# Sixteen experts taken in groups of four in the down product, and the 48 dense chunks of a second stream tied to places among their loads

## The chip, the cores and the metric

One core of a Trainium2 chip. The metric is the device time of one execution in microseconds, the median of several runs. TensorE, VectorE (DVE), ScalarE (ACT), GpSimd (POOL) and the sync engine (SP) each have a queue of their own and work through it in order; sixteen DMA engines carry what SP, POOL and ACT issue.

## The reference, cut to what matters

Two networks one behind the other over 256 tokens of width 1024, all in 32-bit floats. The first has one block: a linear-attention mixer, then a mixture of 16 experts. Each expert picks its own 32 tokens:

```python
gate, idx = lax.top_k(jnp.swapaxes(aff, 1, 2), cap)              # 16 experts, 32 tokens each
xe = h[bidx, idx]
a = jnp.einsum('becd,edf->becf', xe, w_gate)                     # 1024 -> 1408
u = jnp.einsum('becd,edf->becf', xe, w_up)
ye = jnp.einsum('becf,efd->becd', jax.nn.silu(a) * u, w_down) * gate[..., None]
return jnp.zeros_like(h).at[bidx, idx].add(ye)
```

The second network has two layers of four mixers and an MLP (1024 to 4096 and back), on the tokens and on a context of 256 positions of its own. The context's stream does not depend on the first network: its whole first layer, and keys and values of its second, can be computed at any time before the tokens reach the layer that reads them.

## The kernel before, in words

An expert's weights come in loads of 704 KB (128 partitions of 1408 numbers, `load_raw`, L271): eight for gate, eight for up, eight for down. SP issues all 384 in program order into a ring of six buffers (`ringp`); the first 16 go into buffers of their own ahead of the experts (`load_ahead`, L801). SP's order is the program's; the order on every other engine is made by a planner, which walks through the program with a modelled timeline and puts on each engine what is ready there, earlier lines first.

`up_and_gate` (L1045) multiplies an expert's 32 gathered tokens with a load in four products of 352 columns, each of which runs as two instructions, so a load is eight instructions of L1057. The four products go to four strips of 32 columns of the array. Then `sgm` (tanh on ACT, two operations on DVE) and a transpose on DVE give the hidden values `ht` (L1087 to L1091).

The down product (L1095 to L1106) takes eight rounds `c`, one for each 128 output columns. A round is one load: eleven products of 128 columns, 22 instructions of L1101, spread over the four strips and accumulated to four partial sums. ACT evacuates them (`ye`), a product with `ga` (L1105, two instructions) adds the four partial sums, weighs them and scatters the 32 tokens to their 256 places, and DVE adds the result to `xT` (L1106). `ga` is made for each expert: POOL copies the expert's 32 columns of `oa` four times (L1080), TensorE transposes (L1082), ACT evacuates. In the last expert each round also feeds the sums of squares for the next norm (L1110 to L1113).

The context's stream (`ZF`, L1499) stands behind the experts in the program: `layer(ZF, 0, ...)`, then `k_chunk` and `v_chunk` for the second layer (L1501 to L1507). It has 48 calls of `dense` (L287): 10 in the mixers, 4 in their output product, 16 and 16 in the MLP, 2 for the last keys and values. A call has 48 products of 256 columns (L305). Its weights come in two halves of 512 KB, issued on POOL's queue into three buffers (`fr`); ACT splits off the high part (`hi`, L265), DVE or, in the mixers and for keys and values, POOL the low part (`lo`, L267), into three pairs of buffers (`hlp`). As the planner's order goes by what is ready, the context's products come in wherever the experts' products wait, from the first expert on. Its mixers hold long chains on DVE and ACT: 62 taps of a convolution (L1303), softmax, norms.

After the experts the tokens go through the two layers of the second network (`ZC`); these read the context's keys and values.

Of the kernel before, what the change touches and what calls it, by code (L numbers as in the profile page):

```python
# [10 lines left out]
FT = mybir.dt.float32  # L11
# [7 lines left out]
T = 256  # L19
# [84 lines left out]
def layout(inp):  # L104
# [78 lines left out]
    dn = f("w_exp_down")[0].reshape(NE, 128, 11, 8, 128).transpose(0, 3, 1, 2, 4)  # L183
    a["wd"] = np.ascontiguousarray(dn).reshape(NE, 8, 128, RW)
# [20 lines left out]
def build(tc, I, out, dbg=None, upto=99):  # L205
# [35 lines left out]

    def advance(n):

        for _ in itertools.islice(fills[0], n):
            pass
# [41 lines left out]
    def dense(ps, parts, H, act_stationary=False, order=(0, 1), fill=0, late=False, n=0):  # L287

        hh, hl_ = H
        for rnd in ((0, 1), (2,)) if late else ((0, 1, 2),):
            for half in order:
                whi, wlo = parts[half]
                pairs = ((whi, hh), (wlo, hh), (whi, hl_)) if late else ((whi, hh), (whi, hl_), (wlo, hh))
                for k in range(4):
                    kk = half * 4 + k
                    for b in range(2):
                        s = slice(b * 128, (b + 1) * 128)
                        for w, h in (pairs[i] for i in rnd):  # L300
                            if act_stationary:
                                l, r = h[:, kk, s], w[:, k, :]
                            else:
                                l, r = w[:, k, s], h[:, kk, :]
                            PE.matmul(ps[:, b, :], l, r, start=(n == 0), stop=(n == 47), skip_group_check=True)  # L305
                            n += 1
                    if fill and k % 2:
                        advance(fill)

# [735 lines left out]
    def up_and_gate(e):  # L1045
# [5 lines left out]
        for w, ps in ((I["wg"], pg), (I["wu"], pu)):  # L1051
            for k in range(KD):
                if e == 0 and ps is pg and k < KD - 1:
                    gather(k + 1)
                raw = ahead.pop(0) if ahead else load_raw(ZA, w[e, k], RW)
                for j in range(4):
                    PE.matmul(ps[32 * j:32 * j + 32, :], xe[:, k, e * 32:(e + 1) * 32],  # L1057
                              raw[:, j * 352:(j + 1) * 352], start=(k == 0), stop=(k == KD - 1))
# [15 lines left out]
    for e in range(NE):  # L1074
        pg, pu = pgpu if e == 0 else up_and_gate(e)

        pga = pdn.tile([128, 512], FT, name="pga", tag="dn")
        o4 = tb.tile([128, 2, 128], FT, name="o4", tag="o4")
        for a in range(2):
            G.tensor_copy(o4[:, a, :].rearrange("p (j s) -> p j s", j=4),  # L1080
                          oa[:, a, None, e * 32:(e + 1) * 32].to_broadcast([128, 4, 32]))
            PE.transpose(pga[:, a * 128:(a + 1) * 128], o4[:, a, :], ident)  # L1082
        ga = tb.tile([128, T], FT, name="ga", tag="ga")
        evac(ga, pga[:, :T])
# [5 lines left out]
        ht = tb.tile([128, 11, 32], FT, name="ht", tag="ht")  # L1090
        V.transpose(ht, sgm.rearrange("p (q i) -> p i q", i=11))  # L1091
        if e == NE - 1:
            sums = pgu.tile([128, 352], FT, name="sums", tag="pg")

        for c in range(8):  # L1095
            pd = pdn.tile([128, 512], FT, name="pd", tag="dn")
            py, po = pd[:, 0:128], pd[:, 256:512]
            raw = load_raw(ZA, I["wd"][e, c], RW)
            for i in range(11):
                j = i % 4  # L1100
                PE.matmul(py[32 * j:32 * j + 32, :], ht[:, i, :], raw[:, i * 128:(i + 1) * 128], start=(i < 4),  # L1101
                          stop=(i >= 7))
# [4 lines left out]
            if e == NE - 1:  # L1107
# [375 lines left out]
    def layer(Z, l, mod, m, x, norm1=norm):  # L1483
# [16 lines left out]
                x=c2T, np=3, ahead=0, lo=G, fill=0, sc=fms, sct="ms")  # L1500
    ZF.dma.dma_start(c2T.rearrange("p k t -> p (k t)"), I["c2T"])  # L1501
# [5 lines left out]
    v_chunk(ZF, 1, H, vc[1])  # L1507
    phF.close()
# [67 lines left out]
```

## Time and profile before

| | us |
|---|---|
| median of 3 runs | 1938.36 |
| lowest, highest | 1932.96, 1942.03 |
| the profiled execution | 1939.22 |
| its span, first to last instruction | 1937.3 |
| TensorE busy | 1735.1 (90%) |
| DVE busy | 1020.8 (53%) |
| ACT busy | 652.1 (34%) |
| POOL busy | 432.1 (22%) |

Bytes moved: 529.36 MB, on average 273 GB/s. The granted clock of TensorE over the span is 0.919 of full speed. Busy time is a union of overlapping instructions; a busy TensorE is not TensorE at its peak. In a table of stretches, (x...) is the number of instructions, PEld is the loading of stationary operands, "DMA share" the mean busy share of the 16 DMA engines (it can read slightly over 1).

### The profile page before, as it was taken

The numbers are of one execution on the slowest core, as the hardware profiler recorded it, in microseconds if no ns is written. First come the engines' busy times: TensorE is split into PE (matmuls) and PEld (weight loads), VectorE is DVE, ScalarE is ACT, GpSimd is POOL, SyncE is SP. The second block draws the span as 40 slices with busy tenths as digits, with TensorE's granted clock in tenths as the row PEclk, the third lists the DMA queues.
The fourth block names the chain that finished last, engine by engine and source line by source line (L and its number), as shares of the span: only waits on it lengthen the run. The fifth ranks groups of instructions, "written<-read, shape, count | busy, mean of one in ns | idle before, by whom it ended". The sixth has DMA issues, their size and how long they took to land. (4 is left out here: it accounts for less than half of the span.)

```text
span 1937.3 us, 37898 instructions
## 1 busy us (share of the span) xinstructions
PE 1735.1 (90%) x15947; PEld 1353.1 (70%) x15947; DVE 1020.8 (53%) x1892; ACT 652.1 (34%) x1095; POOL 432.1 (22%) x408
## 2 busy tenths in 40 slices
PE   5998998879989999998878777889899999989998
PEld 3776876456667776776533322677899897789997
DVE  5666564556445343434311111538688884867664
ACT  3432332313323222223200000235454343545443
POOL 2334131464321011101200000254411125540000
PEclk8999998889999999999967676789999999999999
DMA  9667887788799999999899999742368863335651
GB/s 356 222 220 241 321 295 258 287 322 286 260 349 344 375 374 360 363 356 367 326 414 414 414 407 413 275 146 89 109 219 319 297 213 96 112 109 163 186 185 66
DMA packets 124232, 529.36 MB, mean 273 GB/s; under 512 B 13917, under 2 KB 14173, under 8 KB 123550
## 3 DMA queue, kind: packets, MB, share of 16 engines
q1 hardware_dynamic: 91086, 405.56, 56.8%
q0 software_dynamic: 32544, 119.16, 17.9%
q8 instruction: 125, 2.05, 0.4%
q10 hardware_dynamic: 432, 2.23, 0.3%
q14 instruction: 45, 0.37, 0.0%
HBM read 525.84 MB, written 1.05 MB: 272 GB/s over the span
## 5 line engine op out<-in xcount | busy, mean ns | idle before, releaser
L265 ACT ACTIVATE hi<-raw 128x1024 fp32r<-128x1024 f32 x316 | 329.4, 1054 | 317.7 <-PE oproj L305 109.8
L267 POOL TENSOR_TENSOR lo<-raw,hi 128x1024 fp32r<-128x1024 f32 x94 | 239.6, 2558 | 471.0 <-ACT hi L265 406.2
L267 DVE TENSOR_TENSOR lo<-raw,hi 128x1024 fp32r<-128x1024 f32 x222 | 273.1, 1243 | 106.4 <-ACT hi L265 104.5
L305 PE MATMUL oproj<-hidh,hi 128*128 128x256 f32 x768 | 218.8, 285 | 8.5 <-ACT hi L265 5.7
L305 PE MATMUL oproj<-hidh,lo 128*128 128x256 f32 x768 | 219.3, 286 | 7.2 <-DVE lo L267 7.2
L305 PE MATMUL oproj<-hidl,hi 128*128 128x256 f32 x768 | 217.8, 284 | 0.0
L305 PE MATMUL pw<-hh,hi 128*128 128x256 f32 x704 | 202.2, 290 | 8.4 <-ACT hi L265 3.1
L305 PE MATMUL pw<-hh,lo 128*128 128x256 f32 x704 | 201.5, 290 | 6.0 <-DVE lo L267 6.0
L305 PE MATMUL pw<-hlo,hi 128*128 128x256 f32 x704 | 194.5, 287 | 1.6 <-DVE hlo L360 1.6
L305 PEld LDWEIGHTS oproj<-hidh,hi 128*128 128x128 f32 x768 | 146.4, 191 | 18.3 <-ACT hi L265 9.8
L305 PEld LDWEIGHTS oproj<-hidh,lo 128*128 128x128 f32 x768 | 146.0, 190 | 14.7 <-DVE lo L267 9.5
L305 PEld LDWEIGHTS oproj<-hidl,hi 128*128 128x128 f32 x768 | 145.8, 190 | 6.9 <-issue 6.9
L1057 PE MATMUL pu<-raw,xe 128*32 128x352 f32 x1024 | 131.7, 599 | 21.1 <-DMA raw<-in_wu_dram 21.1
L1106 DVE SCALAR_TENSOR_TENSOR xT<-pd,mod,xT 128x256 f32<-128x256 f32 x128 | 61.3, 483 | 166.6 <-PE pd L1105 165.9
L305 PEld LDWEIGHTS pw<-hh,hi 128*128 128x128 f32 x704 | 136.3, 194 | 17.4 <-ACT hi L265 5.4
L305 PEld LDWEIGHTS pw<-hh,lo 128*128 128x128 f32 x704 | 136.1, 194 | 12.6 <-DVE lo L267 8.0
L1057 PE MATMUL pg<-raw,xe 128*32 128x352 f32 x1024 | 116.4, 524 | 25.6 <-DMA raw<-in_wg_dram 25.4
L305 PEld LDWEIGHTS pw<-hlo,hi 128*128 128x128 f32 x704 | 132.3, 193 | 9.7 <-issue 7.7
L1101 PE MATMUL pd<-raw,ht 128*32 128x128 f32 x2816 | 115.6, 293 | 20.4 <-DVE ht L1091 10.6
L609 ACT ACTIVATE ye<-pd 128x128 f32<-128x128 f32 x128 | 35.2, 276 | 285.0 <-PE pd L1101 284.7
L1101 PEld LDWEIGHTS pd<-raw,ht 128*32 128x32 f32 x2816 | 88.1, 116 | 53.4 <-issue 28.2
L479 DVE CUSTOM_DVE_ANT_0 raw<-raw,adarow,par 128x1024 f32<-128x1024 f32 x64 | 84.0, 1313 | 59.8 <-DMA raw<-in_ada0x_dram 40.0
(460 smaller groups left out, 3572.8 us busy)
## 6 DMA issues: line engine op xcount, KB each, us to landing
raw<-in_wg_dram SPq DMA_DIRECT2D x128, 704.0 KB, 7.4
raw<-in_wu_dram SPq DMA_DIRECT2D x128, 704.0 KB, 8.4
raw<-in_wd_dram SPq DMA_DIRECT2D x128, 704.0 KB, 7.9
raw<-in_w_dram SPq DMA_DIRECT2D x128, 512.0 KB, 3.9
raw<-in_wi_dram SPq DMA_DIRECT2D x68, 512.0 KB, 5.4
raw<-in_ada_dram POOLq DMA_DIRECT2D x64, 512.0 KB, 4.9
raw<-in_w_dram POOLq DMA_DIRECT2D x64, 512.0 KB, 7.3
raw<-in_ada0x_dram POOLq DMA_DIRECT2D x32, 512.0 KB, 4.9
```

Of the source, the lines that this page charges most:

```text
L265: A.activation(hi, src, AF.Copy, scale=scale)
L267: (eng or V).tensor_sub(lo, src, hi.bitcast(FT))
L305: PE.matmul(ps[:, b, :], l, r, start=(n == 0), stop=(n == 47), skip_group_check=True)
L479: V.tensor_tensor_reduce(raw, raw, row, 1.0, bias[:, 16 + n:17 + n], OP.mult, OP.add, accum_out=mod[:, 0, 16 + n:17 + n])
L609: A.activation(dst, ps, AF.Copy, scale=scale)
L1057: PE.matmul(ps[32 * j:32 * j + 32, :], xe[:, k, e * 32:(e + 1) * 32], raw[:, j * 352:(j + 1) * 352], start=(k == 0), stop=(k == KD - 1))
L1101: PE.matmul(py[32 * j:32 * j + 32, :], ht[:, i, :], raw[:, i * 128:(i + 1) * 128], start=(i < 4), stop=(i >= 7))
L1106: V.scalar_tensor_tensor(xT[:, c, :], po, m0[:, 0, 40 + c:41 + c], xT[:, c, :], op0=OP.mult, op1=OP.add)
```

## The change

The down weights are laid out anew on the host, so that a load holds 11 of the 44 blocks of 128x128 that four experts have for one round. The experts are taken in groups of four: gate and up of all four with their hidden values, then eight rounds of four loads. In a round the four experts' products go to the four strips, 44 in all, so the evacuated tile holds 4 x 32 tokens, and one product with `ga` scatters them. `ga` is now the plain transpose of 128 columns of `oa`; the copies on POOL are gone. `ht` has eight buffers instead of two.

The last TensorE instruction of each of the 384 loads is kept in `steps`. From these 48 are chosen, at loads 8 + 0.92 x n x 376/48, and `issue_after` puts each of the context's 48 calls of `dense` behind its load on TensorE's queue: its products cannot be placed earlier than that instruction. They may be placed later. The loads and splits of the context's weights are not tied.

```diff
-    dn = f("w_exp_down")[0].reshape(NE, 128, 11, 8, 128).transpose(0, 3, 1, 2, 4)
-    a["wd"] = np.ascontiguousarray(dn).reshape(NE, 8, 128, RW)
+    dn = f("w_exp_down")[0].reshape(NE // 4, 4, 128, 11, 8, 128).transpose(0, 4, 2, 3, 1, 5)
+    a["wd"] = np.ascontiguousarray(dn.reshape(NE // 4, 8, 128, 4, RW).transpose(0, 1, 3, 2, 4))
...
+    steps, turns = [], []
...
         hh, hl_ = H
+        es = ExitStack()
+        if turns:
+            es.enter_context(tc.issue_after(turns.pop(0)))
         for rnd in ((0, 1), (2,)) if late else ((0, 1, 2),):
...
+        es.close()
...
-                    PE.matmul(ps[32 * j:32 * j + 32, :], xe[:, k, e * 32:(e + 1) * 32],
-                              raw[:, j * 352:(j + 1) * 352], start=(k == 0), stop=(k == KD - 1))
+                    mm = PE.matmul(ps[32 * j:32 * j + 32, :], xe[:, k, e * 32:(e + 1) * 32],
+                                   raw[:, j * 352:(j + 1) * 352], start=(k == 0), stop=(k == KD - 1))
+                steps.append(mm.ins)
...
-    for e in range(NE):
-        pg, pu = pgpu if e == 0 else up_and_gate(e)
-
-        pga = pdn.tile([128, 512], FT, name="pga", tag="dn")
-        o4 = tb.tile([128, 2, 128], FT, name="o4", tag="o4")
-        for a in range(2):
-            G.tensor_copy(o4[:, a, :].rearrange("p (j s) -> p j s", j=4),
-                          oa[:, a, None, e * 32:(e + 1) * 32].to_broadcast([128, 4, 32]))
-            PE.transpose(pga[:, a * 128:(a + 1) * 128], o4[:, a, :], ident)
-        ga = tb.tile([128, T], FT, name="ga", tag="ga")
-        evac(ga, pga[:, :T])
+    def hidden(pg, pu):
 
         sgm = tb.tile([128, 352], FT, name="sgm", tag="sgm")
         A.activation(sgm, pg, AF.Tanh, scale=0.5)
         V.scalar_tensor_tensor(sgm, sgm, 1.0, pg, op0=OP.add, op1=OP.mult)
         V.tensor_mul(sgm, sgm, pu)
-        ht = tb.tile([128, 11, 32], FT, name="ht", tag="ht")
+        ht = tb.tile([128, 11, 32], FT, name="ht", tag="ht", bufs=8)
         V.transpose(ht, sgm.rearrange("p (q i) -> p i q", i=11))
-        if e == NE - 1:
+        return ht
+
+    for g in range(NE // 4):
+        hts = [hidden(*(pgpu if e == 0 else up_and_gate(e))) for e in range(g * 4, g * 4 + 4)]
+
+        pga = pdn.tile([128, 512], FT, name="pga", tag="dn")
+        for a in range(2):
+            PE.transpose(pga[:, a * 128:(a + 1) * 128], oa[:, a, g * 128:(g + 1) * 128], ident)
+        ga = tb.tile([128, T], FT, name="ga", tag="ga")
+        evac(ga, pga[:, :T])
+        if g == NE // 4 - 1:
             sums = pgu.tile([128, 352], FT, name="sums", tag="pg")
-
         for c in range(8):
             pd = pdn.tile([128, 512], FT, name="pd", tag="dn")
             py, po = pd[:, 0:128], pd[:, 256:512]
-            raw = load_raw(ZA, I["wd"][e, c], RW)
-            for i in range(11):
-                j = i % 4
-                PE.matmul(py[32 * j:32 * j + 32, :], ht[:, i, :], raw[:, i * 128:(i + 1) * 128], start=(i < 4),
-                          stop=(i >= 7))
+            for n in range(44):
+                if n % 11 == 0:
+                    raw = load_raw(ZA, I["wd"][g, c, n // 11], RW)
+                i, j = divmod(n, 4)
+                mm = PE.matmul(py[32 * j:32 * j + 32, :], hts[j][:, i, :], raw[:, n % 11 * 128:(n % 11 + 1) * 128],
+                               start=(i == 0), stop=(i == 10))
+                if n % 11 == 10:
+                    steps.append(mm.ins)
...
-            if e == NE - 1:
+            if g == NE // 4 - 1:
...
+    turns += [steps[8 + int(n * 0.92 * (len(steps) - 8)) // 48] for n in range(48)]
     ZF.dma.dma_start(c2T.rearrange("p k t -> p (k t)"), I["c2T"])
     layer(ZF, 0, mods[1], 1, False)
```

## Rows read from the trace of the kernel before

**Rows 1.** Stretches, all engines: the stretch, its us, busy us (instructions), clock, DMA share, GB/s
```profile
375.00:550.00 175.00, 155.60 (x1465) 112.04 (x1463) 98.57 (x233) 55.54 (x119) 78.56 (x50) 0.93 0.82 294
550.00:955.00 405.00, 377.20 (x3768) 289.86 (x3767) 171.20 (x267) 118.67 (x195) 53.60 (x85) 0.97 0.95 358
955.00:1240.00 285.00, 221.61 (x2228) 88.47 (x2228) 43.58 (x90) 28.28 (x86) 3.52 (x9) 0.71 1.00 406
352.00:1240.00 888.00, 775.25 (x7656) 500.65 (x7654) 322.07 (x619) 212.01 (x418) 147.13 (x159) 0.88 0.94 360
```
**Rows 2.** Stretches, gate and up products (L1057) alone; eight instructions are a load
```profile
352.00:375.00 23.00, 11.23 (x128) 3.38 (x128) 0.98 0.93 328
375.00:550.00 175.00, 28.96 (x268) 6.98 (x272) 0.93 0.82 294
550.00:955.00 405.00, 80.89 (x812) 18.54 (x811) 0.97 0.95 358
955.00:1240.00 285.00, 125.29 (x848) 20.49 (x848) 0.71 1.00 406
```
**Rows 3.** Stretches, down products (L1101) alone; 22 instructions are a load
```profile
375.00:550.00 175.00, 20.12 (x493) 13.50 (x487) 0.93 0.82 294
550.00:955.00 405.00, 39.73 (x1056) 30.41 (x1056) 0.97 0.95 358
955.00:1240.00 285.00, 54.55 (x1232) 43.02 (x1232) 0.71 1.00 406
```
**Rows 4.** Stretches, the products with ga (L1105) alone
```profile
375.00:550.00 175.00, 14.73 (x48) 7.57 (x48) 0.93 0.82 294
550.00:955.00 405.00, 29.83 (x96) 14.63 (x96) 0.97 0.95 358
...
352.00:1240.00 888.00, 83.98 (x256) 42.97 (x256) 0.88 0.94 360
```
**Rows 5.** Stretches, the dense products of the context (L305) alone
```profile
375.00:550.00 175.00, 83.59 (x540) 72.52 (x540) 0.93 0.82 294
550.00:955.00 405.00, 251.48 (x1764) 224.19 (x1764) 0.97 0.95 358
```
**Rows 6.** Two windows of 25 us, all engines
```profile
625.00:650.00 25.00, 22.37 (x185) 15.99 (x185) 9.30 (x13) 7.11 (x8) 2.24 (x5) 0.93 1.01 394
1050.00:1075.00 25.00, 19.99 (x250) 10.27 (x246) 5.18 (x10) 2.60 (x9) 0.53 (x2) 0.77 1.02 413
```
**Rows 7.** DMA queues from 550 to 955 (packets, MB, share), landing there, and from 975
```profile
q1 hardware_dynamic: 21454, 107.42, 70.2%
q0 software_dynamic: 10161, 36.97, 24.8%
...
raw<-in_wu_dram SPq DMA_DIRECT2D x52, 704.0 KB, 6.4
...
raw<-in_wu_dram SPq DMA_DIRECT2D x48, 704.0 KB, 9.0
```
**Rows 8.** Timelines of TensorE, POOL and DVE near 420: start, us, operation, count [idle before]
```profile
418.97 0.28 PE L305 MATMUL pvv<-hi,hh 128*128 128x256 f32 x1
...
419.33 0.28 PE L305 MATMUL pvv<-hi,hh 128*128 128x256 f32 x1
...
431.44 0.58 PE L305 MATMUL pvv<-lo,hh 128*128 128x256 f32 x1 [10.98 <-POOL lo L267]
...
416.45 14.94 POOL L267 TENSOR_TENSOR lo<-raw,hi 128x1024 fp32r<-128x1024 f32 x1 [5.55 <-ACT hi L265]
...
410.11 19.09 DVE L1303 SCALAR_TENSOR_TENSOR ya<-glu,par,ya 128x256 f32<-128x256 f32 x48
```
**Rows 9.** Timeline of TensorE, a load's products at half and at full clock
```profile
488.36 1.23 PE L1057 MATMUL pg<-raw,xe 128*32 128x352 f32 x8
...
491.07 0.80 PE L1057 MATMUL pg<-raw,xe 128*32 128x352 f32 x8
```
**Rows 10.** Timelines of SP's queue and TensorE at the experts' end
```profile
1221.96 4.61 SPq L273 DMA_DIRECT2D raw<-in_wd_dram  x3
...
1238.24 1.19 PE L1105 MATMUL pd<-ga,ye 128*128 128x256 f32 x4
```

More of the change, by code (lines that the diff above doesn't have):

```diff
@@ L1507, in build @@
     v_chunk(ZF, 1, H, vc[1])
+    assert not turns
     phF.close()
```

## The prediction

> **What bounds the kernel now.** I read a table of stretches over the experts first, to see which engine is short in each; then the same table for single lines, the DMA queues, and the timelines at the worst stall. The experts run from 352 to 1240 us, 888 of the 1937.3 us [rows 1]. Nothing before 352 is changed, and what follows 1240 starts from the same data. Inside, DMA is busy 0.94 of the time, TensorE 775 us, and 319.7 MB arrive (888 us at 360 GB/s) [rows 1]: 384 expert loads of 0.721 MB less the 16 loaded ahead, and the context's 96 loads of 0.524 MB.
>
> Three stretches behave differently. From 375 to 550 the context's mixers stand between the experts: 540/48 = 11.25 dense chunks, 268/8 + 493/22 = 56 expert loads consumed, DMA share 0.82, 294 GB/s [rows 1 to 3, 5]. From 550 to 955 its MLP and last keys: 36.75 chunks, 149.5 loads, share 0.95, 358 GB/s, with TensorE busy 377 of 405 us [rows 1 to 3, 5]. From 955 to 1240 the experts are alone: 162 loads in 285 us, 1.76 us each, with 413 GB/s in a window of it [rows 1 to 3, 6]. So the end is pure DMA while TensorE has room, and the first two stretches lose DMA time because TensorE holds the buffers. The loads in flight show that: 6.4 us to landing at 107.42 MB in 405 us is 1.7 MB, 2.4 loads of the ring's six, against 9.0 us at 413 GB/s, 5.2 loads, when the experts are alone [rows 6, 7].
>
> **The change, part by part.** *Groups of four.* The down products keep their number and size. The products with ga (L1105) fall from 256 instructions to 64: 192 at 29.83/96 = 0.311 us is 60 us of TensorE at full clock, but 256 - 48 - 96 = 112 of the 256 lie in the stretch where DMA hides them [rows 4]. Gone as well are 96 evacuations, 96 updates of xT, 24 of 32 transposes, 32 copies on GpSimd. All lie on engines with room (DVE is busy 322 of 888 us, ACT 212, POOL 147 [rows 1]), so they count as nothing; if that cover were gone they would matter only at the end of a group. The wait of the down products for ht comes four times, not sixteen. The next expert's gate products go on while the hidden values are made; pu is free again eight loads before it is written. The new buffers for ht cost space only. On SP's queue the loads are as many and as large, 64 for gate and up, then 32 for down: nothing.
>
> *The 48 chunks.* Chunk n may start behind load 8 + 7.2n, the last behind load 354 of 384. Queued behind a chunk on TensorE are expert products, and behind those SP's next load. The context's loads on POOL's queue and the splits on ACT, DVE and POOL are not held by the edit; they run ahead until three raw halves and three hi/lo pairs are full, then wait. On DVE an expert's sgm work can stand behind such a split; its reader is eight loads away, some 18 us, which covers it. The context ends 30 loads, about 53 us, before the experts do, so the next layer should find its keys.
>
> *The price of a period.* A chunk and 7.2 loads are 5.19 + 1.05 = 6.24 MB. At 413 GB/s this is 15.1 us, at 358 it is 17.4. The trace has no such mix (POOL's bytes are 17% of it; they were 26% from 550 to 955 and nothing at the end), so I go between: 358/0.95 = 377 GB/s at a full share, 406/1.00 alone [rows 1, 7], and two thirds of the way from alone to that mix gives 386, hence 16.2 us. A window in the mixed stretch reached 394 at a share of 1.01 [rows 6], which is why I trust this end more than 358. TensorE needs, per period, 7.2 × 0.80 = 5.8 us for loads [rows 9], 48 products 0.12 us apart, 5.8 us [rows 8], and 0.4 us for L1105 (64 × 0.311/48): 12.0 us. From 550 to 955 its need by the same prices was 4.1 × 0.80 + 5.8 + 0.8 = 9.9 us a chunk and it took 405/36.75 = 11.0, a ninth more; with that 13.3 us. That is less than 16.2: TensorE waits for DMA, and DMA is the bound.
>
> *The mixers.* Their worst loss is 11 us at 420, when TensorE waits for a GpSimd split that took 14.94 us, while DVE ran taps for 19 us without a pause [rows 8]. Chunks one after another leave no time for that; with 7.2 loads between them such a split is ready in time. The taps, the softmax chains and the turns at half clock after a wait [rows 9] stay. In the same 11.25 chunks 73 loads now go by, not 56. By bytes that is 64.4 MB/386 = 167 us. By TensorE it is 175 + 17 × 0.80 = 189, less the stall's 11 and three quarters of L1105's 14.7 us [rows 4], 167 again if both gains are whole and 189 if none is; I take 178, the middle.
>
> *The end.* The last three down loads are issued at 1222 to 1226.6, but the last product with ga ends at 1239.4, since one expert's down products wait for its ht and then run eight rounds [rows 10]. With four loads a round only the last round stands behind the last load: 7 us less.
>
> **The sum.** Before: 23 + 175 + 405 + 285 = 888. After: 23 (16 loads [rows 2]) + 178 (73 loads) + 265 loads with 36.75 chunks, 229.6 MB/386 = 595, + 30 loads at 1.76 less 7 = 46: 842 us. That is 46 less. The profiled execution took 1939.2 (span 1937.3 and 1.9 around it), 0.9 over the median of the three, so **1893 us**.
>
> Bounds: mixers 167 to 189; the long stretch from 574 us (400 GB/s, a little over that best window) to 641 (358). All good ends together give 23 + 167 + 574 + 46 = 810, 1861 us; all bad ones 23 + 189 + 641 + 53 = 906, 1957 us.
>
> A rule speaks against any gain. The Trainium skill ("DMA: Bandwidth & Descriptors", Specifications) gives a limit of about 358 GB/s from HBM for one core; by it 319.7 MB need 893 us and spreading gains nothing. This case's trace disagrees: 413 GB/s over 25 us and 406 over 285 us [rows 1, 6], and the measurement decides.
>
> **Rivals.** *DMA full from 375 on.* If the grouped experts leave TensorE so much room that the mixers' stalls are absorbed too, the good ends hold: 810 to 825, 1861 to 1876. For it: 13.3 us of TensorE in 16.2. Against it: taps, softmax and norm chains are as long as before.
>
> *The mix itself is slow.* If 358 GB/s belongs to two queues sharing the engines, not to held buffers, then spreading makes more of the stage mixed: 23 + 178 + 641 + 46 = 888, 1939 us, no change. For it: SP's own packets move 107.42 MB in 0.702 × 405 us, 378 GB/s, against 406 alone [rows 1, 7]. Against it: the 2.4 loads in flight, and the window at 394.
>
> *The planner bunches.* The turns are lower bounds only; the order on TensorE is planned against a modelled clock. If chunks pile up behind their turns, the stage looks as now and only the grouping counts: the 44.6 us of L1105 in the first two stretches [rows 4] shrink by three quarters, 33 us, and since DMA is nearly as short there (shares 0.82 and 0.95), I give half of it to the time: about 1923. For it: now too the planner sets the places. Against it: a chunk gets room among 7.2 loads where 4.1 were enough.
>
> *The clock falls* (the slower side). In the experts-alone stretch the granted clock is 0.71, in the crowded one 0.97 [rows 1]; with TensorE waiting for DMA between chunks the dense chunks would run at 1.2 GHz part of the time, where a load's products take 1.23 us, not 0.80 [rows 9]. TensorE becomes the bound once the mean clock is under 13.3/16.2 = 0.82. At 0.75, a little over the figure of the experts alone, a period is 13.3/0.75 = 17.7 us, the stage 23 + 189 + 651 + 46 = 909, **1960 us**. Against it: a TensorE that is the bound has no gaps, and the clock returns. The Trainium skill ("TensorE: Matmul & The Clock Gate", Loop structure matters more than you think) says that a loop which waits for DMA between matmuls runs them at the low clock; this rule would have the clock fall here, and the two clocks above agree with it.
>
> **How the numbers follow.** Forecast 0.50; DMA full from 375 on 0.14; planner bunches 0.13; the mix itself is slow 0.12; the clock falls 0.11. The range 1861 to 1944 leaves out the clock rival, the upper part of the slow mix and what would beat all good ends: under 2 in 10. A change of 0.5%, 9.7 us, is about what a measurement of this kernel can tell from none. Faster by more than that: forecast, full DMA and most of the bunching, 0.75. Within: most of the slow mix and the rest of the bunching, 0.14. Slower: the clock rival, 0.11.
>
> **What would show it.** Right: chunks of the context spread to about 50 us before the experts' end; 64 instructions of the product with ga; a DMA rate of 380 to 395 GB/s all through the MLP's part, with more than three loads in flight; the mixers without an 11 us gap; the experts' last product near 1194. Wrong: a rate near 358 with full queues (the mix), a granted clock under 0.8 with TensorE busy throughout (the clock), dense chunks still thick in the first half (the planner), or keys that the next layer waits for.

## The result, and the profile after

The changed kernel takes **1889.43 us** (median of four runs, 1879.52 to 1894.91) against 1937.43 for the kernel before on the same chip: a ratio of 0.9746, 95% interval 0.97 to 0.9793. 1893 was predicted. The profiled execution took 1888.94 us.

The page of the changed kernel: the span, TensorE's busy time, and four rows of the 40 slices (47 us each).

```profile
span 1887.2 us, 37071 instructions
PE 1657.1 (88%) x15731; PEld 1323.3 (70%) x15731; DVE 975.2 (52%) x1796; ACT 626.4 (33%) x987; POOL 419.7 (22%) x376
...
PE   5999998796988888887888887599999999999997
PEclk7999998898999979889898898798999999989999
DMA  9566887797999999999999999432378853335551
GB/s 374 197 224 215 335 292 263 268 395 271 345 360 405 412 400 401 405 401 413 412 405 405 400 352 414 159 121 67 113 268 308 295 181 124 97 107 183 186 185 62
```

From the twelfth slice to the last whole one before the experts' end, 352 to 414 GB/s stand in a row. Before, that rate came only after 955 [rows 1]. The stretches, with the columns of [rows 1] (busy us of PE, PEld, DVE, ACT, POOL, clock, DMA share, GB/s):

```profile
356.00:376.00 20.00, 20.00 (x168) 9.13 (x166) 5.40 (x10) 9.19 (x17) 9.32 (x9) 0.95 0.92 317
376.00:542.00 166.00, 143.82 (x1358) 96.45 (x1357) 88.41 (x233) 47.38 (x94) 72.96 (x43) 0.92 0.88 334
542.00:1125.00 583.00, 496.37 (x5182) 340.97 (x5178) 174.19 (x259) 119.97 (x175) 48.84 (x75) 0.90 1.01 402
1125.00:1187.00 62.00, 40.65 (x752) 28.43 (x746) 5.92 (x15) 9.45 (x20) 4.23 (x2) 0.89 0.95 380
356.00:1187.00 831.00, 700.84 (x7448) 474.98 (x7446) 273.91 (x515) 185.99 (x306) 135.35 (x128) 0.90 0.98 384
```

The same table for the context's dense products alone (L312 here, L305 before), busy us and instructions of PE and PEld:

```profile
376.00:542.00 166.00, 72.48 (x480) 64.03 (x480) 0.92 0.88 334
542.00:1125.00 583.00, 271.14 (x1824) 245.16 (x1824) 0.90 1.01 402
1125.00:1187.00 62.00, 0.00 (x0) 0.00 (x0) 0.89 0.95 380
```

So 10 chunks lie in the mixers' stretch and 38, evenly, in the long one; the last 62 us are experts alone. TensorE is idle 87 of the 583 us and the DMA engines hardly ever. What TensorE waits for shows it too: the waits of its instructions from 352 to 1210, us in total, times, longest:

```profile
PE pg L1065 <- DMA raw<-in_wg_dram: 39.9, 34, 2.1
PE pd L1112 <- DMA raw<-in_wd_dram: 30.9, 31, 2.1
PE pu L1065 <- DMA raw<-in_wu_dram: 17.9, 14, 2.3
PE zin L312 <- POOL lo L271: 9.3, 1, 9.3
```

89 us of waiting for expert loads, and one long wait for GpSimd. The DMA queues from 550 to 1075 (packets, MB, share) and the loads issued there (KB, us to landing), to be read beside [rows 7]:

```profile
q1 hardware_dynamic: 35279, 176.63, 83.1%
q0 software_dynamic: 9792, 35.66, 17.7%
...
raw<-in_wg_dram SPq DMA_DIRECT2D x88, 704.0 KB, 10.6
raw<-in_wu_dram SPq DMA_DIRECT2D x85, 704.0 KB, 10.6
```

176.63 MB in 525 us is 336 GB/s; times 10.6 us that is 3.6 MB, by this estimate 4.9 loads of the ring's six in flight, where 2.4 were before. By its share, SP's queue moves 176.63 MB in 0.831 x 525 us, 405 GB/s: as much as the experts alone did, though POOL's bytes are 17% of the whole.

**Where the 50 us went.** From here on the stage is the time from the start of the first gate product to the start of the last product with ga. It was 886.6 us (352.5 to 1239.1) and is 826.8 (356.4 to 1183.2): 59.8 less. But the stage began 3.9 us later in this execution, and from the last product with ga to the span's end it takes 704.0 us instead of 698.2: 5.8 given back where nothing was changed. 59.8 - 3.9 - 5.8 = 50.1, the difference of the spans. The 3.9 are no cost of the change: nothing before the stage was edited, and over the fourteen profiles of this document it begins between 347.9 (e9) and 362.8 us (e11).

### The profile page after: what moved, and what is told of

Read it like the earlier page. It is cut to its first block, busy times and chain, and to the rows that moved or that the text cites. A ratio compares the mean times of both kernels' runs of the same rounds, so it can differ in the third digit from the quotient of the medians.

```text
span 1887.2 us, 37071 instructions
## 1 busy us (share of the span) xinstructions
PE 1657.1 (88%) x15731; PEld 1323.3 (70%) x15731; DVE 975.2 (52%) x1796; ACT 626.4 (33%) x987; POOL 419.7 (22%) x376
## 5 line engine op out<-in xcount | busy, mean ns | idle before, releaser
L312 PE MATMUL oproj<-hidh,hi 128*128 128x256 f32 x768 | 225.2, 293 | 1.8 <-DVE xT L911 1.5
L312 PE MATMUL oproj<-hidl,hi 128*128 128x256 f32 x768 | 222.1, 289 | 0.0
L312 PE MATMUL oproj<-hidh,lo 128*128 128x256 f32 x768 | 221.3, 288 | 0.0
L312 PE MATMUL pw<-hh,hi 128*128 128x256 f32 x704 | 205.1, 294 | 3.6 <-ACT relu L1479 1.6
L312 PE MATMUL pw<-hh,lo 128*128 128x256 f32 x704 | 201.6, 289 | 0.0
L312 PE MATMUL pw<-hlo,hi 128*128 128x256 f32 x704 | 194.8, 287 | 1.7 <-DVE hlo L368 1.7
L312 PEld LDWEIGHTS oproj<-hidh,hi 128*128 128x128 f32 x768 | 151.1, 197 | 24.0 <-issue 21.2
L312 PEld LDWEIGHTS pw<-hh,hi 128*128 128x128 f32 x704 | 137.6, 196 | 24.8 <-issue 18.4
L312 PEld LDWEIGHTS oproj<-hidh,lo 128*128 128x128 f32 x768 | 150.4, 196 | 3.9 <-issue 3.8
L312 PEld LDWEIGHTS oproj<-hidl,hi 128*128 128x128 f32 x768 | 150.7, 196 | 3.1 <-issue 3.1
L1065 PE MATMUL pg<-raw,xe 128*32 128x352 f32 x1024 | 108.5, 510 | 40.3 <-DMA raw<-in_wg_dram 39.9
L312 PEld LDWEIGHTS pw<-hh,lo 128*128 128x128 f32 x704 | 137.5, 195 | 6.5 <-issue 6.5
L1112 PE MATMUL pd<-raw,ht 128*32 128x128 f32 x2816 | 110.8, 286 | 34.0 <-DMA raw<-in_wd_dram 30.9
L312 PEld LDWEIGHTS pw<-hlo,hi 128*128 128x128 f32 x704 | 134.0, 195 | 4.8 <-issue 2.7
L277 POOL DMA_DIRECT2D raw<-in_w_dram x64 | 33.8, 528 | 463.7 <-DVE lo L271 463.7
L1112 PEld LDWEIGHTS pd<-raw,ht 128*32 128x32 f32 x2816 | 80.5, 113 | 58.8 <-DMA raw<-in_wd_dram 35.3
L1065 PE MATMUL pu<-raw,xe 128*32 128x352 f32 x1024 | 103.8, 503 | 17.9 <-DMA raw<-in_wu_dram 17.9
L312 PE MATMUL zin<-hh,lo 128*128 128x256 f32 x272 | 81.2, 301 | 9.3 <-POOL lo L271 9.3
## 6 DMA issues: line engine op xcount, KB each, us to landing
raw<-in_wg_dram SPq DMA_DIRECT2D x128, 704.0 KB, 9.4
raw<-in_wu_dram SPq DMA_DIRECT2D x128, 704.0 KB, 9.5
raw<-in_wd_dram SPq DMA_DIRECT2D x128, 704.0 KB, 9.9
```

Of the source, the lines that this page charges most:

```text
L277: Z.dma.dma_start(raw[:p, :n], src)
L1065: mm = PE.matmul(ps[32 * j:32 * j + 32, :], xe[:, k, e * 32:(e + 1) * 32], raw[:, j * 352:(j + 1) * 352], start=(k == 0), stop=(k == KD - 1))
L1112: mm = PE.matmul(py[32 * j:32 * j + 32, :], hts[j][:, i, :], raw[:, n % 11 * 128:(n % 11 + 1) * 128], start=(i == 0), stop=(i == 10))
```

## The experiments

Theory: the loads in flight set the rate. Where dense chunks stand close, TensorE holds the ring's buffers; with even turns the ring stays full. Grouping helps by leaving TensorE less to do. The rivals are named at each. Stage is that of one profiled execution each, and rest is what comes behind it to the span's end. The kernel before, measured anew beside each set of variants, had medians of 1937 to 1953 us, so each median has its ratio to the one beside it.

| kernel | median us | ratio [95%] | stage us | rest us |
|---|---|---|---|---|
| before | 1937.43 | 1 | 886.6 | 698.2 |
| changed | 1889.43 | 0.9746 [0.97, 0.9793] | 826.8 | 704.0 |
| e1_group_only | 1920.54 | 0.9864 [0.9833, 0.9896] | 862.2 | 708 |
| e2_turns_only | 1922.09 | 0.9872 [0.9842, 0.9901] | 855.3 | 716 |
| e3_split_on_dve | 1874.00 | 0.965 [0.9604, 0.9697] | 813.2 | 701.1 |
| e4_four_ga | 1884.61 | 0.9687 [0.9659, 0.9716] | 826.7 | 705.7 |
| e5_lagged_down | 1897.55 | 0.9752 [0.9688, 0.9816] | 837.9 | 700.9 |
| e6_four_rounds | 1904.79 | 0.9784 [0.9717, 0.985] | 847.9 | 705 |
| e7_front | 1905.21 | 0.9781 [0.9712, 0.9849] | 847.2 | 699.8 |
| e8_wide_mixers | 1876.80 | 0.9627 [0.9553, 0.9701] | 806.1 | 713.2 |
| r9_after_again | 1886.91 | 0.9681 [0.9631, 0.973] | 831.4 | 707.7 |
| e9_gain_kept | 1872.59 | 0.9612 [0.9575, 0.9649] | 827.6 | 693.7 |
| e10_split_gain | 1864.75 | 0.9568 [0.9532, 0.9605] | 815.9 | 696.7 |
| e11_wide_gain | 1868.21 | 0.9583 [0.9543, 0.9624] | 808.5 | 705.1 |

Two things limit what the table can tell. The changed kernel has the ratio 0.9746 in one set and 0.9681 (r9) in another, with nearly the same median, so ratios of different sets compare to no better than some 0.007, or 13 us. And four profiles of what is in effect the same stage (the changed kernel, r9, e9, and e4, as is shown below) have 826.7 to 831.4 us for it, so a few us of stage decide nothing.

### Each half alone

e1 is the changed kernel without its turns:

```diff
-    turns += [steps[8 + int(n * 0.92 * (len(steps) - 8)) // 48] for n in range(48)]
```

> The changed kernel without the turns: experts in groups of four, the 48 dense chunks wherever the planner finds room. Theory A (the gain comes from spreading the chunks, so that loads stay in flight; the grouping only takes 60 us of TensorE that were mostly hidden): the chunks end again near 60% of the loads, DMA share about 0.95 while they last, total 1915 to 1928 us. Theory B (the grouping is the gain, since sixteen waits and 96 products with ga go): 1885 to 1900 us, and the turns add nothing.

e2 is the kernel before with the turns, its experts one by one:

```diff
+            steps.append(mm.ins)
...
+    turns += [steps[8 + int(n * 0.92 * (len(steps) - 8)) // 48] for n in range(48)]
```

> The kernel before with the turns alone: every expert its own down product and its 16 products with ga a round pair, the 48 chunks behind loads 8 + 7.2n. Theory A: TensorE needs 7.2 x 0.80 + 5.8 + 1.6 = 13.2 us a period, a ninth more is 14.6, still under the 15.5 us that DMA takes at 403 GB/s, so most of the gain stays: 1892 to 1908 us. Theory B (the grouping is the gain): 1925 to 1940 us.

e1's 1920.54 is as the theory said; e2's 1922 is not, it had 1892 to 1908. Part of that miss lies behind the stage (a rest of 716 us against 698.2 before), and is shown with e8. The stages are 24.4 and 31.3 us under the kernel before, 55.7 together, against 59.8 for both at once: the two halves nearly add, and neither is the whole. Two stretches of e1, then the same of e2 (columns as in the stretches above):

```profile
625.00:675.00 50.00, 47.73 (x411) 33.78 (x410) 17.50 (x22) 11.50 (x13) 5.30 (x10) 0.97 1.02 412
800.00:850.00 50.00, 46.23 (x594) 37.93 (x596) 17.29 (x22) 13.34 (x20) 4.77 (x9) 1.00 0.96 355
```

```profile
650.00:750.00 100.00, 86.54 (x939) 60.31 (x935) 33.00 (x47) 21.69 (x38) 7.95 (x17) 0.97 1.01 404
750.00:850.00 100.00, 86.58 (x948) 59.60 (x941) 34.51 (x49) 23.47 (x41) 8.23 (x16) 0.97 1.01 408
```

In e1 TensorE is busy 92 to 95% and the rate swings between 355 and 412; in e2 it has 13% to spare and the rate holds at 404 to 408, with an old-style down product. The mix of two queues is therefore not slow in itself. The two stretches of e1 show it best, since POOL's queue has 27% of the bytes in both, about the 26% of the long stretch before. Their DMA queues and loads, first from 625 to 675, then from 800 to 850:

```profile
q1 hardware_dynamic: 2977, 14.91, 72.9%
q0 software_dynamic: 1546, 5.64, 28.5%
...
raw<-in_wg_dram SPq DMA_DIRECT2D x11, 704.0 KB, 11.6
raw<-in_wu_dram SPq DMA_DIRECT2D x10, 704.0 KB, 8.6
```

```profile
q1 hardware_dynamic: 2592, 12.94, 71.5%
q0 software_dynamic: 1296, 4.72, 23.3%
...
raw<-in_wd_dram SPq DMA_DIRECT2D x11, 704.0 KB, 6.1
```

By the sum used above, some 3.6 to 4.8 expert loads are in flight in the first and 2.2 in the second; SP's queue moves 409 GB/s at its full share there and 362 here. With the same mix, the rate goes with the loads in flight. What e2 lacks beside the changed kernel, 28.5 us of stage, is the next question.

### Is it TensorE's time for the product with ga?

Where grouping makes one product with ga, e4 makes it four times over (the same result, three times for nothing):

```diff
-            PE.matmul(po, ye, ga, start=True, stop=True)
+            for _ in range(4):
+                PE.matmul(po, ye, ga, start=True, stop=True)
```

> The changed kernel with each product with ga run four times into the same place, so that TensorE has the 192 instructions (60 us at full clock) back that the grouping took away, and nothing else changes. Theory A (DMA is the bound, TensorE has some 2 us of room in a period): 0 to 6 us more, 1889 to 1896 us. Theory B (TensorE's work is the bound, and the 60 us are the gain): 20 us more or above, 1910 us and over.

The products with ga in the stage, first of the changed kernel, then of e4:

```profile
356.00:1187.00 831.00, 23.10 (x64) 0.90 0.98 384
```

```profile
356.00:1187.00 831.00, 66.44 (x256) 0.93 0.97 382
```

43 us more of TensorE, and the stage is 826.7 instead of 826.8. The "60 us of L1105" of the prediction were hidden whole, in the mixers too, once the turns are in: here grouping does not help by leaving TensorE less to do. Whether some of e1's 24.4 us, without turns and with TensorE busy 92 to 95%, is TensorE's time was not tried.

### The wait for ht, or the work of the rounds?

e5 is e2 with each expert's down product one expert later, so that no down product stands right behind its own hidden values; it keeps the 128 rounds:

```diff
-    for e in range(NE):
-        pg, pu = pgpu if e == 0 else up_and_gate(e)
...
+    for e in range(NE):
+        ht = hidden(*(pgpu if e == 0 else up_and_gate(e)))
+        if late is not None:
+            down(e - 1, late)
+        late = ht
+    down(NE - 1, late)
```

> The kernel with the turns alone (every expert its own down product), with the down product of an expert taken one expert later, behind the gate and up products of the next: its hidden values are then made while other expert products run. Sixteen evacuations, products with ga and updates of xT per pair of experts stay. Theory C (what the grouping gives beside the turns is the wait for ht, sixteen in place of four, with what queues behind it): ratio to the kernel before 0.970 to 0.980, as the whole change. Theory D (it is the work of the rounds on ACT, DVE and GpSimd, 96 evacuations, 96 updates and 32 copies that stand in line with the context's splits): 0.984 to 0.990, as with the turns alone.

e6 is the changed kernel with the work of four rounds in each round (three evacuations, three products with ga and three updates into scratch, the old copies on GpSimd and eight transposes a group):

```diff
...
             evac(ye, py, 0.5)
-            PE.matmul(po, ye, ga, start=True, stop=True)
+            for _ in range(3):
+                yx = tb.tile([128, 128], FT, name="yx", tag="yx", bufs=1)
+                evac(yx, py, 0.5)
+            for _ in range(4):
+                PE.matmul(po, ye, ga, start=True, stop=True)
+            for _ in range(3):
+                xx = tb.tile([128, T], FT, name="xx", tag="xx", bufs=1)
+                V.scalar_tensor_tensor(xx, po, m0[:, 0, 40 + c:41 + c], xT[:, c, :], op0=OP.mult, op1=OP.add)
```

> The changed kernel with all the work of the old rounds back: in each round four evacuations, four products with ga and four updates (three of each into places that nobody reads), in each group the old copies on GpSimd, eight transposes. The waits for ht stay at four. Theory D (the work of the rounds is what the grouping saves): ratio 0.982 to 0.990. Theory C (the waits): 0.970 to 0.978, no different from the change.

By their ratios e5 (0.9752) lies where theory C had it, and e6 (0.9784) lies between the ranges of the two theories; the intervals are too wide to decide. By the stage e5 wins 17.4 of the 28.5 us and e6 loses 21.1, together more than the whole. The waits show why e5's gain is not one thing. Of TensorE's waits in e2:

```profile
PE pvv L311 <- POOL lo L270: 11.0, 1, 11.0
...
PE pd L1109 <- issue: 7.3, 4, 2.3
PE pd L1109 <- DVE ht L1099: 6.7, 4, 3.7
...
PE pd L1109 <- DVE nwta L255: 2.2, 1, 2.2
```

The three rows of the down products are one wait: all nine of these instructions start within 0.15 us of the end of an ht. For one that the view puts down to "issue", the timelines of DVE and TensorE:

```profile
986.70 0.79 DVE L1099 STREAM_TRANSPOSE ht<-sgm 128x352 f32<-128x352 f32 x1
...
987.59 0.75 PE L1109 MATMUL pd<-raw,ht 128*32 128x128 f32 x16 [2.27 <-issue]
```

So e2 waits 16.2 us for ht, where the changed kernel waits 2.0 and e5 shows no such row. The first row is the GpSimd stall, which the changed kernel still has (9.3 us) and e5 has not (0.6), for a reason that is shown with the stall below. What the stall is worth in the stage is told by e3 below: 13.6 us, and 11.7 in e10. If it is 10 to 13 here, e5's 17.4 leave 4 to 7 us for the wait for ht, though TensorE waits 14 us less; with e6's 21.1 for the work of the rounds that makes 25 to 28 of the 28.5. This is a sum of stages that are good to some 5 us each, and not a test: no run has the later down products with the stall kept. Nor is e6 quite the old work: its four evacuations, products and updates stand one behind another in one round and on one tile pd, where the old kernel had one set to a load. The rounds' work shows in the stretch from 560 to 1120, first of the changed kernel, then of e6:

```profile
560.00:1120.00 560.00, 477.89 (x4915) 326.51 (x4915) 170.89 (x253) 116.18 (x168) 45.35 (x72) 0.90 1.01 401
```

```profile
560.00:1120.00 560.00, 482.29 (x4968) 337.74 (x4964) 197.57 (x311) 127.10 (x222) 43.16 (x71) 0.93 1.00 396
```

DVE has 27 us more, ACT 11, and the rate is 396, though DVE is busy 35% and ACT 23%. That the small operations delay what stands behind them on DVE and ACT is the likely way, but it is not shown: TensorE's waits for expert loads fall from 89 to 70 us, and no single wait on DVE or ACT grows by more than 4 us. Which of the two engines' extra work does it was not tried apart.

### The spread

e7 has the same turns over the first 60% of the loads:

```diff
-    turns += [steps[8 + int(n * 0.92 * (len(steps) - 8)) // 48] for n in range(48)]
+    turns += [steps[8 + int(n * 0.60 * (len(steps) - 8)) // 48] for n in range(48)]
```

> The changed kernel with the 48 turns spread over the first 60% of the loads, 4.7 loads a chunk, as dense as the kernel before had them. Theory A (spreading lets TensorE fall short of DMA's pace): TensorE needs 4.7 x 0.80 + 5.8 + 0.4 = 10 us, 11 with the usual ninth, against 4.7 x 1.75 + 2.6 = 10.8 us of DMA, so TensorE holds the buffers again while the chunks last and the last 40% run on DMA alone: ratio 0.982 to 0.990, near the grouping alone. Theory E (any tie of a chunk to a load helps, by keeping the context's splits ahead of its products): 0.972 to 0.980.

The stage is 20.4 us longer than the changed kernel's, though every turn is still a turn; but it is also 15.0 us shorter than e1's, which has no turns, and the ratio 0.9781 lies in theory E's range and not in A's. So of the 35.4 us that the turns give the grouped kernel the distance between the chunks makes some 20, and a tie at the old density some 15; what the tie does there was not tried. From 376 to 542 the rate falls to that of the grouping alone, 302; from 542 to 1125 it is 397, against e1's 387:

```profile
376.00:542.00 166.00, 145.22 (x1187) 101.65 (x1186) 90.44 (x210) 48.23 (x94) 75.04 (x44) 0.90 0.84 302
```

### The stall in the mixers

The prediction had this stall vanish; here it is in the changed kernel, in the timelines of POOL, DVE and TensorE:

```profile
422.22 13.25 POOL L271 TENSOR_TENSOR lo<-raw,hi 128x1024 fp32r<-128x1024 f32 x1 [4.43 <-ACT hi L269]
...
412.36 20.91 DVE L1316 SCALAR_TENSOR_TENSOR ya<-glu,par,ya 128x256 f32<-128x256 f32 x43
...
435.52 0.58 PE L312 MATMUL zin<-hh,lo 128*128 128x256 f32 x1 [9.31 <-POOL lo L271]
```

A split that takes 2.4 us elsewhere lasts until 435.47, and DVE's run of 43 taps ends at 433.27, 2.2 us earlier: the split did its work after the run. In [rows 8] it is the same, 431.39 and 429.20. The Trainium skill ("SBUF — State Buffer", Who interferes with whom) says that a DVE instruction with two inputs in SBUF contends with a GpSimd instruction that reads SBUF, and that the one which comes second waits; the taps read glu and ya, and the trace agrees. It shows more: the run is 43 instructions, and the split is let in behind the last of them, not between two. In e5, updates of xT break the run of taps, each with a pause of 0.3 us, and there no split takes more than 3.4 us. e3 moves the context's splits to DVE:

```diff
-                x=c2T, np=3, ahead=0, lo=G, fill=0, sc=fms, sct="ms")
+                x=c2T, np=3, ahead=0, lo=None, fill=0, sc=fms, sct="ms")
```

> The changed kernel with the low parts of all the context's weights made on DVE, none on GpSimd. Theory A (the 9.3 us wait of TensorE in the mixers is a GpSimd operation slowed by DVE's run of taps, 13.3 us in place of 2.4): no split over 1.5 us, the wait shrinks below 3 us, the stage is 5 to 12 us shorter, 1877 to 1885 us. Theory B (the split is late because it stands behind the chain that ends in those taps, whatever engine makes it): it now waits on DVE behind up to 20 us of taps, the wait is as long or longer, 1888 to 1900 us.

The splits on GpSimd from 356 to 1187 (min, median, max ns), first of the changed kernel, then of e3 with its mixers' stretch:

```profile
L271 POOL TENSOR_TENSOR lo<-raw,hi x30: 2333/2377/13249, 360.6 to 1185.1; 128x1024 fp32r<-128x1024 f32 x30
```

```profile
L271 POOL TENSOR_TENSOR lo<-raw,hi x5: 2349/2352/2407, 1165.4 to 1184.6; 128x1024 fp32r<-128x1024 f32 x5
...
376.00:542.00 166.00, 148.00 (x1521) 103.39 (x1517) 100.84 (x236) 50.84 (x99) 14.28 (x24) 0.95 0.96 365
```

365 GB/s instead of 334 in the mixers, and 13.6 us less of stage, a little over the 9.3 us of the wait and the 5 to 12 expected; e10 against e9, the same step further below, gives 11.7. e8 adds to e3 wider turns for the mixers, one chunk in nine loads:

```diff
-    turns += [steps[8 + int(n * 0.92 * (len(steps) - 8)) // 48] for n in range(48)]
+    turns += [steps[16 + 9 * n if n < 10 else 106 + (n - 10) * 248 // 38] for n in range(48)]
```

> The changed kernel with the low parts on DVE, and the ten chunks of the mixers nine loads apart (from load 16), the other 38 then 6.5 apart up to load 354. If the mixers lose DMA time because their chains fill 7.2 loads' time, wider turns give it back: the mixers' stretch at 390 GB/s and over, the MLP's still at 400 (TensorE 12.7 of 13.9 us), the whole 8 to 15 us under the run with splits on DVE, ratio 0.957 to 0.962. If they lose it to chains that TensorE waits for wherever they stand, nothing: 0.963 to 0.968.

Its stage is 7 us shorter still (382 GB/s in the mixers, under the 390 expected), but the rest is 12 us longer, and the total the same. Three stretches of 10 us of e8's second layer, some 430 us behind the stage:

```profile
1570.00:1580.00 10.00, 10.00 (x80) 9.52 (x80) 4.40 (x5) 4.15 (x5) 8.92 (x5) 1.00 0.69 197
...
1590.00:1600.00 10.00, 10.00 (x32) 7.05 (x31) 6.06 (x14) 5.36 (x13) 0.00 (x0) 0.50 0.18 54
1600.00:1610.00 10.00, 10.00 (x30) 7.27 (x31) 5.75 (x11) 2.35 (x4) 1.88 (x1) 0.50 0.00 1
```

For some 30 us the granted clock is 0.50, the lower level (1.2 GHz), with TensorE busy throughout; before it, it had been busy 10 of 10 us at 1.00. e2 has such a stretch at the same place of its second layer, and over the 100 us around it both have 0.85, the others 0.97 to 0.99. In both, TensorE had gone over just before from dense products to mostly score products (psc) with operands of 32 rows. e3 has these products there too and reads 0.90 and 0.93 in its two windows of 10 us, so what sets the fall off stays open. At half clock 30 us cost 15 at most, an estimate that covers e8's 12 us (against e3) and most of e2's 18 (against the kernel before): these long rests come for the most part from the clock there, not from what the edits do to the experts. Whether the executions that were not profiled have it is not known.

### What was given back behind the stage

From the last product with ga to the first convolution product of the next layer it is 26.8 us before and 39.3 after. The next layer first splits xT times its gain (preh). These eight operations on ACT before, ns and first to last start:

```profile
L374 ACT ACTIVATE preh<-xT,gain x8: 492/493/494, 1227.9 to 1240.5; 128x256 fp32r<-128x256 f32 x8
```

and after, with the line of the timeline that shows what they wait for:

```profile
L382 ACT ACTIVATE preh<-xT,gain x8: 494/498/508, 1194.6 to 1197.5; 128x256 fp32r<-128x256 f32 x8
...
1194.65 3.31 ACT L382 ACTIVATE preh<-xT,gain 128x256 fp32r<-128x256 f32 x8 [8.18 <-DVE gain L1543]
```

Before, they ran between the last updates of xT, the last one right behind the last update, at 1240.5. After, all wait until 11 us past the last product with ga (1183.2), for a gain of eight columns, which DVE computes behind the whole norm. Nothing in the diff names it. But ht now has eight buffers and o4 is gone, so the pools of the next layer come to lie on other temporaries of the experts, and the gain, as I read it, must wait for one that the norm still uses. Three kernels give it a place in the permanent pool:

```diff
-        g1 = mod_gain(Z.h, mod, m, 1, P(f"n1_{l}"), "g1")
+        g1 = mod_gain(Z.h if norm1 is norm else pz, mod, m, 1, P(f"n1_{l}"), "g1" if norm1 is norm else "g1z")
...
-        gain2 = Z.h.tile([128, 8], FT, name="gain2")
+        gain2 = gain
```

r9 is the changed kernel beside them; e9 it with this edit, e10 also with the splits of e3, e11 also with the turns of e8.

> The changed kernel itself once more, so that the next three have it beside them on the same chip. Expected by every theory: 1880 to 1897 us, the stage of the experts 825 to 833 us, and 702 to 706 us from the last weighted product of the experts to the end, the first convolution product of the next layer about 39 us behind that last product.

> The changed kernel with the next layer's eight-column gain in a place of its own in the permanent pool; in the changed kernel that gain lies where a temporary of the experts lay, and is written only after it. Theory P (the gain's place is what moved the next layer's first splits behind the norm): the splits run between the last eight updates of xT again, the first convolution product comes 25 to 29 us after the last weighted product instead of 39, and the part behind the experts is 6 to 11 us shorter than the changed kernel's 704. Rival Q (the next layer's first weights land late, since the ring is still full of the last loads): the splits come early but the convolution stays at 36 to 40 us and the part behind the experts within 2 us of 704.

> The gain in its own place, and the context's low halves on VectorE instead of GpSimd. If both effects are real and lie in different stretches, they add: the stage of the experts 811 to 816 us, the part behind it 692 to 698, so 1862 to 1872 us with the profile's execution near the middle, 14 to 24 us under the changed kernel. If the gain's place is worth nothing at the end (rival Q), 1870 to 1878.

> As the kernel before it, with ten turns nine loads apart for the context's mixers and the other 38 spread over the rest. Its stage alone was 806 us against 813 with the even turns; the part behind was 713 against 701. If the part behind is set by the gain's place, it falls to 695 to 703 here and the total is 1862 to 1870; if its 713 comes from something else that these turns push behind the stage, it stays over 707 and the total over 1873.

In e9 the splits start before the stage ends:

```profile
L382 ACT ACTIVATE preh<-xT,g1z x8: 492/493/496, 1125.2 to 1177.7; 128x256 fp32r<-128x256 f32 x8
```

The rest is 693.7 us, 10 under the changed kernel's 704.0 and 14 under r9's 707.7, and the median 14.3 under r9's; the intervals of the two ratios still touch. The convolution starts 33.1 us behind the last product, not the 25 to 29 expected: prel, the low halves on DVE, is still placed behind the norm (1186.8). So the gain's place is what holds the splits back; that it would bring the old order back whole was wrong, for 6.2 of the 12.5 us before the convolution come back. The 10 to 14 us of the whole rest are less sure: r9's profiled execution, 1897.56 us, is the slowest of its six, and the kernels with late splits and no fall of the clock have rests from 699.8 (e7) to 708. e10 has both gains: stage 815.9, rest 696.7, **1864.75 us**, 22 us under r9 with intervals apart (0.9532 to 0.9605, 0.9631 to 0.973). It beats both kernels. e11's rest is 705.1, just over the 695 to 703 expected (its clock is 0.98 where e8's was 0.85; its profiled execution, 1878.12, is the slowest of six), and its time is that of e10 within the intervals: of the 7.4 us that the wide turns gain in the stage nothing is left at the end, and why was not settled.

## Why the prediction was right, and where its terms were off

The time came out 4 us under the forecast, by the mechanism named: even turns and a DMA rate near that of the experts alone. That it came so near is luck in part, as the sum at the end of the parts shows. By parts, on the windows of the sum (stage from 352 or 356 to the end of the last product with ga, 888 before, 842 predicted, 828 measured):

**The long stretch** was 595 us for 229.6 MB at 386 GB/s. It had 271.5 loads and 38 chunks, 235.5 MB, in 583 us: 404 GB/s. The mix rate was mis-sized: at 386 these bytes take 610 us, so this term alone was 27 us too long. The step that failed is the interpolation between 377 at a full share and 406 alone. The 377 was taken as a price of mixing two queues; SP's queue now does 405 at a full share in a mix with 17% of POOL's bytes, and in e1 409 with 27%. With 2.4 loads in flight (2.2 in e1's slow stretch) a DMA engine counts as busy and yet moves less; with 4.9 it does not.

**The mixers** were 178 us for 73 loads and 11.25 chunks. They took 166 for 65 loads and 10 chunks; at the predicted 362 GB/s these 57.4 MB take 159, so 7 us too short. The step "such a split is ready in time" failed: the stall kept 9.3 of its 11 us, because it hangs on DVE's taps and not on the distance of the chunks. Removing it gave 13.6 us (e3), more than the 11 that the prediction counted for it.

**The end** was 46 us for 30 loads with 7 us gained; it is 59 for 32 (1125 to 1183.6), where 32 x 1.76 - 7 gives 49; 2 us over the loads alone, so the gain of 7 did not come at all. The timelines of SP's queue and TensorE, to set beside [rows 10]:

```profile
1150.98 21.19 SPq L277 DMA_DIRECT2D raw<-in_wd_dram  x13
...
1182.91 0.70 PE L1118 MATMUL pd<-ga,ye 128*128 128x256 f32 x2 [1.74 <-ACT ye L617]
```

The last down load is issued by 1172.2, 11.4 us before the last product with ga ends, 12.9 before the change. One round behind the last load is right, but the load itself, with some 9 us to landing before and after, takes most of that time, and the seven rounds that were to be saved had been hidden behind it.

**Outside the stage** the prediction had nothing: "what follows 1240 starts from the same data". The data are the same and their places are not. The rest took 5.8 us longer here; by e9 the places cost 10 to 14, of which 6.2 lie before the first convolution product.

Together: 3 us less at the start, 27 less, 7 and 9 more, against 842: 828, as measured. So the stage alone was 14 us better than forecast, and 10 us outside it, where the forecast had nothing (3.9 of a later start, 5.8 of the rest), took most of that back. The misses cancel. (One sum of the prediction has a slip on which nothing hangs: the loads that it names make 315.6 MB, not 319.7.)

**The rivals.** A slow mix fell by the 405 GB/s, and by e1's 412 in a mix as rich as that of the kernel before. The planner did not bunch: 301 to 331 dense instructions lie in each 100 us from 550 to 1050. DMA full from 375 on did not come (0.88 in the mixers), though e3 comes to 0.96. The clock fell as the rival said, from 0.97 to 0.90 in the long stretch, not under the 0.82 from which it decides; TensorE is busy 0.85 of that stretch, against 13.3 of 16.2 predicted. What the prediction held against this rival, that the clock returns where TensorE has no gaps, is not always so: e2 and e8 have 30 us at 0.50 with TensorE busy throughout. The Trainium skill's rule ("TensorE: Matmul & The Clock Gate", Loop structure matters more than you think) points the right way; here it shows no cost, since TensorE waits for loads (89 us) and 43 us more of work on it cost nothing (e4).

**Where the gain lies between the parts.** The prediction put the grouping's work at nothing, "on engines with room". With the turns in, TensorE's share was nothing (e4). The rest was not: 28.5 us of stage lie between e2 and the changed kernel. e6 gives 21 of them to the work of the rounds, with DVE busy 35% and ACT 23%; the wait for ht, which the prediction counted down from sixteen to four without a price, has the 4 to 7 that e5 leaves when the stall is taken off. This division is summed up and not tested.

## What to carry to other kernels

A low rate at a high DMA share can be a ring too empty rather than a limit: count the loads in flight (us to landing times rate) before pricing a mix. An engine's small operations can cost time while the engine has room (e6), so "it has room" needs a test or the wait list beside it; and in that list, rows of one instruction put down to different causes may be one wait. After changing the buffers of one stage, compare the order of the first instructions of the next, since their tiles may have come to lie on other memory.

## What the runs showed of the hardware

One core read at 401 to 413 GB/s over each 100 us from 550 to 1050, with two queues. The Trainium skill ("DMA: Bandwidth & Descriptors", Specifications) lists about 358 as the limit for one core, half of what two share; no stretch here with a full ring, from a program on one core, was held to that. A DMA share near 1 does not say that the rate is reached: e1 has 355 GB/s at 0.96 with 2.2 loads in flight and 412 at 1.02 with some 4, in the same mix. A GpSimd split is held for as long as DVE runs taps without a pause: 13 to 15 us instead of 2.4, in every kernel here that leaves these splits on GpSimd but e5, where the run is broken. And 30 us at half clock came with TensorE busy all the time (e2, e8), some 430 us behind the stage; such a stretch costs as much as many a change gains, so a total alone would have hidden what these two edits do.
